# Three users of two PSUM banks in the expert stage of a hybrid decoder layer: one bank each for tables, layout products and turned halves

## The chip, the cores and the metric

The kernel runs on one core of a Trainium2 chip. The metric is the device time of one launch in microseconds. A core has a matrix engine (TensorE, rows "PE" for its multiplications and "PEld" for its weight loads), a vector engine (VectorE, "DVE"), a scalar engine (ScalarE, "ACT"), GpSimd ("POOL") and SyncE ("SP"), and 16 DMA engines that move data between HBM and the on-chip memory SBUF. Each engine works through its own list of instructions in order. TensorE writes its results to PSUM, a small memory of eight banks, each of 512 float32 values in every one of 128 partitions. VectorE and ScalarE read and write PSUM too.

## The reference, cut to what matters

One layer of a decoder for 512 prompt tokens and 64 sample tokens, width 2048. After a mixing block come the experts, the part that the change touches:

```
def peer(h, w_q, sub_keys, expert_u, expert_v):      # h: tokens x 2048
    ...
    q = (xb @ w_q).reshape(PEER_BLOCK, PEER_HEADS, 2, HALF_DIM)
    sc = jnp.einsum('thpk,pnk->thpn', q, sub_keys)
    v1, i1 = lax.top_k(sc[:, :, 0], PEER_TOPK)
    v2, i2 = lax.top_k(sc[:, :, 1], PEER_TOPK)
    ...                                              # the best 16 of the 256 pairs, for each of 8 heads
    g = jax.nn.softmax(top, axis=-1)
    act = jax.nn.gelu(jnp.einsum('td,thkd->thk', xb, expert_u[eidx])) * g
    return jnp.einsum('thk,thkd->td', act, expert_v[eidx])
```

Each token picks 128 of 16384 experts, and an expert is one row of `expert_u` and one of `expert_v`, each of 2048 float32 values.

## The kernel before

**Stages.** The first third computes the modulation, the projections, the two convolutions, the scan and the output projection. Then come the queries and the choice of experts. The rest is two long loops. The U loop (`for n in range(NU2)`, L2029, 144 rounds) multiplies all prompt tokens with 72 blocks of 128 experts each from the u table; the V loop (L2141) does the same with the v table, weighted. 48 of the 72 blocks (`NF`) are whole blocks of the table, taken by how often they are picked; the other 24 are put together from lists of single experts. Picks that fall into no block, and those of the sample tokens, are computed row by row: 198 gathered tiles of 128 u rows (one row of 2048 values for each of 128 partitions), each multiplied and summed against the tokens on VectorE (`dot`, L1553 to L1559), and as many of v rows.

**A half block.** Each block is two half blocks, so round `n` stands for block `i = n // 2` and half `c = n % 2`. `u_half` (L1691) issues 24 matmuls of 128x512, eight values of `kk` with three products each (high part times high, high times low, low times high, to keep float32 accuracy). The two halves of a block accumulate in one bank, `pu`, taken from a pair of banks with the tag "u". After the second half ScalarE applies gelu to the bank (L1710) and sends the result to HBM. The half block's data `raw` are split into high and low parts by ScalarE (`xhi`, L997) and GpSimd (`xlo`, L998). `ahead(n + 3, n + 2)` at the top of round `n` asks for the load of half block n+3 and splits half block n+2.

**Turned halves.** The 24 listed blocks arrive through an indirect DMA that GpSimd issues (`fetch_x`, L949, after `u_half` of round n for half block n+5, into two buffers `nat`), with experts in the partitions, and have to be turned. `turn_x` (L955) does so inside `u_half` of round n for half block n+3: two 128x128 transposes on TensorE, then a copy by ScalarE to `raw`, at `kk` = 1, 3, 5 and 7. This happens from round 93 on.

**Layout products.** For the V loop every prompt token's 128 gate weights are laid out as a table of 72 blocks x 128 experts. `g_pair` (L1964) makes one-hot operands for eight tokens on VectorE: `ops` compares the table `gk["o"]` with each pick's number inside its block (L1979), `eq` compares the table `gk["w"]` with the pick's block (L1980), and three products with the weights `gk["wq"]` give `wr` (L1982). All three tables lie in PSUM. `g_mm` (L1985) multiplies them, 12 small matmuls for four tokens, into `gk["g"]`, and `g_out` (L1994) has ScalarE copy the result to `stg`, which goes to HBM. `g_one` (L2022) calls both, at the top of a round and at `kk` = 2, 4 and 6, for pairs that were made at least one round earlier.

**Which bank holds what.** `g_start` (L1948) takes the two banks with the tag "g". The bank `kb` holds the tables `o` and `w` and the layout products `g`. The bank `tb` (named "tpbank") holds the weights `wq` and the turned halves `tp`. The program framework puts in the waits between engines: two accesses of one PSUM tile on different engines, which fill the same bank, are kept in the order of the program, whether or not they touch the same columns. The order on each engine is the one written here (`manual_schedule`, L1081), and the shares of each kind of work per round come from constants (`PIECE_G`, `RATE`, `PAIRS`, `LAG`).

Of the kernel before, what the change touches and what calls it, by code (L numbers as in the profile page):

```python
# [11 lines left out]
AF = mybir.ActivationFunctionType  # L12
# [21 lines left out]
L = 72  # L34
# [30 lines left out]
WP = 3  # L65
# [32 lines left out]
def build(ctx, tc, A, O, dbg=None):  # L98
    nc = tc.nc
    V, S, PE, G = nc.vector, nc.scalar, nc.tensor, nc.gpsimd  # L100
# [21 lines left out]
    ident = const.tile([128, 128], F32, name="ident")  # L122
# [302 lines left out]
    for n in ("lru_wa", "lru_wx"):  # L425
        g = wk.tile([128, KW, 64], F32, name=f"g_{n}")
# [28 lines left out]
    def project(src, nm):  # L455
        his, los = stream_w(src, nm)
        p = pp.tile([128, 2, 512], F32, name=f"pp_{nm}", tag="pp")
        mm3([p[:, 0, :HT], p[:, 1, :HT]], his, los, movs)
        return p
# [183 lines left out]
    for k in range(KD):  # L643
        if k < 2:
            out_half(k, 1)
            p = p_out[k]
        else:
            p = project(A["w_out"][k], f"o{k}")
# [25 lines left out]
    def pbank(tag, nm, bufs):  # L674
        return psum["p"].tile([128, 512], F32, name=nm, tag=tag, bufs=bufs)
# [7 lines left out]
    for q in range(4):  # L683
        modulate(x1, R, None, 3, 4 * q, 4, "h2")
        mm3(pq0, *w_q, movs, range(4 * q, 4 * q + 4))
        t = adap.tile([128, 4, 512], F32, name=f"h2s{q}", tag="wa")
# [202 lines left out]
    def new_row(nm):  # L889
        s_ = free_slot()  # L890
        if s_ is None:
            s_ = min(range(slots_now[0]), key=lambda x: held_by[x])
        k = held_by[s_] = len(row_log)
        row_log.append(False)
        return (gp if s_ < RB else pools["vx"]).tile([128, D], F32, name=nm, tag=f"row{s_}", bufs=1), k
# [4 lines left out]
    for i in range(RB):  # L900
        r, k = new_row(f"row0_{i}")
# [35 lines left out]
    nat = {}  # L937
    raws, parts, gsb, ahl, acts, pools = {}, {}, {}, {}, {}, {}
# [16 lines left out]
    def turn_x(n, a):  # L955
        if n not in nat:
            return
        if a == 0:
            k = n % 3
            raws[n] = (ws if k < 2 else wx).tile([128, 8, 128], F32, name=f"raw{n}", tag="wraw", bufs=2 if k < 2 else 1)  # L960
        tp = gk["tp"] if "tp" in gk else pbank("g", f"tp{n}_{a}", 2)[:, :256]
        src = nat[n] if a < 3 else nat.pop(n)
        for k in range(2):
            PE.transpose(tp[:, k * 128:(k + 1) * 128], src[:, (2 * a + k) * 128:(2 * a + k + 1) * 128], ident)  # L964
        S.activation(raws[n][:, 2 * a:2 * a + 2, :], tp.rearrange("p (k c) -> p k c", c=128), AF.Copy)

    def load(n):
        if n >= len(stream):
# [292 lines left out]
    def look():  # L1261

        lp = pools.get("lp")
        if lp is None or "acc" not in lk:
            return
        if lk["feat"] and (len(lk["feat"]) > 1 or lk["next"] >= lk["lim"]):
            j, f = lk["feat"].pop(0)
            reg = lk["acc"][:, 0:256].rearrange("p (d r w) -> p d r w", d=4, w=8)
            for z in range(QT):
                PE.matmul(reg[:, :, 4 * (j % 2) + z, :], f[:, z * 128:(z + 1) * 128], lk["tab"], start=True, stop=True)  # L1270
            if j % JC == 0:
                lk["ev", j // JC] = lp.tile([128, 4, 4 * JC, 8], BF16, name=f"ev{j // JC}", tag="ev", bufs=2)
            if j % 2:
                S.activation(lk["ev", j // JC][:, :, 4 * (j % JC) - 4:4 * (j % JC) + 4, :], reg, AF.Copy)
                lk["done"] = j + 1
        if lk["next"] < lk["lim"]:
            j = lk["next"]
            lk["next"] += 1
            PE.matmul(lk["bc"], lk["one"][:, j:j + 1].to_broadcast([128, 128]), lk["kT", j // 64], start=True, stop=True)
            f = lp.tile([128, NA], F16, name=f"ft_{j}", tag="feat", bufs=3)  # L1280
            S.activation(f, lk["bc"], AF.Sign, bias=lk["bias"])
            lk["feat"].append((j, f))
# [179 lines left out]
    def pick_keys(R, nm, pool, iota1, b):  # L1462

        kk = pool.tile([128, 3, NPK], F32, name=f"kk{nm}", tag="kk", bufs=1)
        b = b.bitcast(U32).rearrange("p (a k) -> p a k", a=2)
        V.tensor_scalar(b[:, 0, :], R[:, 1, :].bitcast(U32), 16, None, op0=ALU.logical_shift_right)
        V.tensor_scalar(b[:, 1, :], R[:, 1, :].bitcast(U32), 65535, None, op0=ALU.bitwise_and)
        V.tensor_copy(kk[:, 1:, :], b)
        for a in range(3):
            V.scalar_tensor_tensor(kk[:, a, :], iota1, 65536.0 if a else 16384.0, kk[:, a, :] if a else R[:, 0, :],  # L1470
                                   op0=ALU.mult, op1=ALU.add)
            V.scalar_tensor_tensor(kk[:, a, :], R[:, 0, :], 0.5, kk[:, a, :], op0=ALU.is_gt, op1=ALU.mult)
        return kk
# [207 lines left out]
    fin = {}  # L1681
# [3 lines left out]
    def mid(n):  # L1685
        for f in mids.pop(n, ()):
            f()
        if R1 is not None and "o" in gk:
            g_one(n)

    def u_half(n, i, c):  # L1691
        hi, lo = parts.pop(n)
        if c == 0:
            fin["pu"] = pbank("u", f"pu{i}", 2)
        pu = fin["pu"]
        for kk in range(8):
            k = 8 * c + kk
            if kk < LK:
                look()
            if kk % 2:  # L1700
                turn_x(n + 3, kk // 2)
            if kk in (2, 6) and R1 is not None and "o" in gk:
                g_one(n)
            if kk == 4:
                mid(n)
            for a, (st, mv) in enumerate(((hi, 0), (hi, 1), (lo, 0))):
                PE.matmul(pu, st[:, kk, :], movA[mv](k), start=k == 0 and a == 0, stop=k == KD - 1 and a == 2)  # L1707
        if c == 1:
            act = actp.tile([128, NA], F32, name=f"act{i}", tag="act", bufs=2)
            S.activation(act, pu, AF.Gelu_apprx_tanh)  # L1710
            nc.scalar.dma_start(actd[V_AT[i] // SG][:, V_AT[i] % SG, :], act)
# [3 lines left out]
    def v_column(n, gi, q, bl, first, last, kq):  # L1715

        k = q * (KD // VQ) + kq
        if first:
            pvs[k] = pbank("ug"[kq // 2], f"pv{gi}_{k}", 2)
        pv = pvs[k]  # L1720
        end = gi == len(GROUPS) - 1
        for j, i in enumerate(bl):
            hi, lo = parts[n + j // 2]
            ah, al = ahl[i]
            hi, lo = (x.rearrange("p (a k) c -> p a k c", a=2)[:, j % 2, kq, :] for x in (hi, lo))
            for a, (st, mv) in enumerate(((hi, ah), (hi, al), (lo, ah))):
                PE.matmul(pv, st, mv, start=first and j == 0 and a == 0,  # L1727
                          stop=last and not end and j == SG - 1 and a == 2)
        if end:
            for t in range(QT):  # L1730
                PE.matmul(pv[:, t * 128:(t + 1) * 128], fin["tok"][t][:, k * 128:(k + 1) * 128], ident,  # L1731
                          start=False, stop=t == QT - 1)
        return k, pv
# [208 lines left out]
    gk = {}  # L1942
# [5 lines left out]
    def g_start():  # L1948

        kb = pbank("g", "kb", 2)  # L1950
        tb = pbank("g", "tpbank", 2)
        cw = pools["rg"].tile([128, 4, L, 2], BF16, name="cw", tag="eq", bufs=1)[:, 0]
        co = pools["rg"].tile([128, 4, 128, 2], BF16, name="co", tag="op", bufs=PAIRS // 2)[:, 0]
        S.activation(cw, nd["ordr"][:, :, None].to_broadcast([128, L, 2]), AF.Copy)
        S.activation(co, iota[:, :, None].to_broadcast([128, 128, 2]), AF.Copy)
        S.activation(kb[:, :128], co.rearrange("p i t -> p (i t)").bitcast(F32), AF.Copy)
        S.activation(kb[:, 128:128 + L], cw.rearrange("p i t -> p (i t)").bitcast(F32), AF.Copy)
        gk["o"] = kb[:, :128].bitcast(BF16).rearrange("p (i b) -> p i b", b=2)
        gk["w"] = kb[:, 128:128 + L].bitcast(BF16).rearrange("p (i b) -> p i b", b=2)
        gk["g"] = kb[:, 128 + L:128 + 5 * L]  # L1960
        gk["wq"] = tb[:, 256:256 + 64 * WP].rearrange("p (w t) -> p w t", w=WP)
        gk["tp"] = tb[:, :256]

    def g_pair(b):  # L1964

# [56 lines left out]
    def g_one(n):  # L2022
        nonlocal spare
        if n >= R1 + FIRST_G and gm[1] < min(upto(n - LAG), gm[2]):
            g_out(gm[1], g_mm(gm[1]))
            gm[1] += 1
            spare += 0.4

    for n in range(NU2):  # L2029
        _, i, c = stream[n]  # L2030
# [110 lines left out]
    for m in range(M):  # L2141
        gi, q, bl, first, final = steps[m]
        n = NU2 + 2 * m
# [4 lines left out]
        for kq in range(KD // VQ):  # L2148
# [9 lines left out]
            if (m, kq) in tplan:  # L2158
                t = len(fin["tok"])
# [5 lines left out]
            k, pv = v_column(n, gi, q, bl, first, final, kq)  # L2165
# [33 lines left out]
    with tc.If(any_ > 0), tc.tile_pool(name="fb", bufs=1) as fp:  # L2199
        io1 = fp.tile([128, 128], F32, name="f_io1")  # L2200
        V.tensor_scalar(io1, iota, 1.0, None, op0=ALU.add)
        for i, (p0, n, c) in enumerate(GT):
# [7 lines left out]
            kb = fp.tile([128, 2 * NPK], F32, name=f"kbf{i}", tag="kb", bufs=1)  # L2210
            kk = pick_keys(R_, f"f{i}", fp, io1, kb)
            w = kk[:, 1, :]
# [9 lines left out]
            a = fp.tile([128, D], F32, name=f"f_a{i}", tag="a", bufs=1)  # L2222
# [105 lines left out]
```

## Time and profile before

| | us |
|---|---|
| median of 3 runs | 3469.14 (3460.91 to 3477.18) |
| the profiled execution | 3474.89 |
| its span, first to last instruction | 3473.0 |
| TensorE matmuls busy | 3087.6 (89%) |
| VectorE busy | 2120.8 (61%) |
| GpSimd busy | 1801.5 (52%) |
| ScalarE busy | 1052.9 (30%) |

In the views of the trace a row names a line of the kernel, the engine and what it writes from what it reads. "Idle" is the time in which that engine had stood still just before the instruction, and the name behind the arrow is the instruction whose end released it; "issue" stands there where the profile shows no releaser. A view by stretches gives, for each stretch of the span in microseconds, every engine's busy time, the clock that TensorE was granted (1 is full speed), the share of time that the DMA engines were busy and the rate at which data moved. Matmuls overlap in TensorE, so that the sum of their durations says less than the distance from one start to the next.

### The profile page before, as it was taken

The numbers are of one execution on the slowest core, as the hardware profiler recorded it, in microseconds if no ns is written. First come the engines' busy times: TensorE is split into PE (matmuls) and PEld (weight loads), VectorE is DVE, ScalarE is ACT, GpSimd is POOL, SyncE is SP. The second block draws the span as 40 slices with busy tenths as digits, with TensorE's granted clock in tenths as the row PEclk, the third lists the DMA queues.
The fourth block names the chain that finished last, engine by engine and source line by source line (L and its number), as shares of the span: only waits on it lengthen the run. The fifth ranks groups of instructions, "written<-read, shape, count | busy, mean of one in ns | idle before, by whom it ended". The sixth has DMA issues, their size and how long they took to land. (4 is left out here: it accounts for less than half of the span.)

```text
span 3473.0 us, 48158 instructions
## 1 busy us (share of the span) xinstructions
PE 3087.6 (89%) x18277; PEld 2535.7 (73%) x18277; DVE 2120.8 (61%) x3550; ACT 1052.9 (30%) x1540; POOL 1801.5 (52%) x1136
## 2 busy tenths in 40 slices
PE   6999999999999899798877777778889998988997
PEld 3788889999899886567766655556667876767776
DVE  3456321232458879787866645555657777877765
ACT  3344211232332336552222333333332221211122
POOL 2333333443432353346534434345679988888872
PEclk8999999999999999899988888799999999999998
DMA  9644566533331264458865766567989999989994
GB/s 389 245 140 141 199 208 213 168 117 133 108 103 62 74 217 171 140 170 309 318 248 191 274 202 203 170 220 274 368 289 381 395 382 406 377 338 384 353 341 159
DMA packets 270862, 831.74 MB, mean 239 GB/s; under 512 B 32476, under 2 KB 70236, under 8 KB 222332
## 3 DMA queue, kind: packets, MB, share of 16 engines
q0 software_dynamic: 73728, 437.74, 33.5%
q1 hardware_dynamic: 132960, 313.27, 26.1%
q10 hardware_dynamic: 63936, 77.61, 6.4%
q8 instruction: 144, 2.36, 0.3%
q14 instruction: 94, 0.77, 0.1%
HBM read 806.49 MB, written 62.61 MB: 250 GB/s over the span
## 5 line engine op out<-in xcount | busy, mean ns | idle before, releaser
L998 POOL TENSOR_TENSOR xlo<-raw,xhi 128x1024 fp32r<-128x1024 f32 x288 | 697.0, 2432 | 486.8 <-ACT xhi L997 466.1
L1586 DVE SCALAR_TENSOR_TENSOR accB<-v,dots,accB 128x2048 f32<-128x2048 f32 x186 | 437.7, 2353 | 186.9 <-DMA v<-v,rows 185.7
L1707 PE MATMUL pu<-hhi,xhi 128*128 128x512 f32 x1152 | 542.5, 471 | 0.0
L997 ACT ACTIVATE xhi<-raw 128x1024 fp32r<-128x1024 f32 x288 | 302.1, 1058 | 783.9 <-PE pv L1727 293.2
L1559 DVE SCALAR_TENSOR_TENSOR u<-u,hT 128x2048 f32<-128x2048 f32 x198 | 447.6, 2281 | 129.7 <-DMA u<-u,rows 116.9
L1727 PE MATMUL pv<-ahi,xhi 128*128 128x512 f32 x1152 | 468.7, 407 | 51.7 <-DVE acc L1749 43.9
L1727 PE MATMUL pv<-ahi,xlo 128*128 128x512 f32 x1152 | 465.0, 404 | 17.5 <-POOL xlo L998 17.4
L1707 PE MATMUL pu<-hlo,xhi 128*128 128x512 f32 x1152 | 479.7, 416 | 0.0
L1707 PE MATMUL pu<-hhi,xlo 128*128 128x512 f32 x1152 | 478.3, 415 | 0.0
L1727 PE MATMUL pv<-alo,xhi 128*128 128x512 f32 x1152 | 463.6, 402 | 0.0
L1727 PEld LDWEIGHTS pv<-ahi,xhi 128*128 128x128 f32 x1152 | 222.4, 193 | 113.4 <-issue 35.4
L1727 PEld LDWEIGHTS pv<-ahi,xlo 128*128 128x128 f32 x1152 | 222.0, 193 | 77.8 <-POOL xlo L998 25.6
L1707 PEld LDWEIGHTS pu<-hhi,xlo 128*128 128x128 f32 x1152 | 233.8, 203 | 55.7
L1707 PEld LDWEIGHTS pu<-hhi,xhi 128*128 128x128 f32 x1152 | 235.5, 204 | 44.4 <-issue 8.6
L1707 PEld LDWEIGHTS pu<-hlo,xhi 128*128 128x128 f32 x1152 | 236.9, 206 | 34.8
L1727 PEld LDWEIGHTS pv<-alo,xhi 128*128 128x128 f32 x1152 | 222.8, 193 | 51.0
L1531 POOL DMA_INDIRECT v<-v,rows x198 | 208.6, 1053 | 57.6 <-issue 40.6
L1531 POOL DMA_INDIRECT u<-u,rows x198 | 205.2, 1036 | 60.9 <-issue 26.0
L964 PE MATMUL tpbank<-ident,nat 128*128 128x128 f32 x384 | 83.7, 304 | 131.2 <-issue 108.4
L1979 DVE TENSOR_TENSOR op<-kb,kw 128x1024 bf16<-128x1024 bf16 x64 | 44.1, 690 | 252.7 <-ACT stg L1998 252.7
L964 PEld LDWEIGHTS tpbank<-ident,nat 128*128 128x128 f32 x384 | 55.3, 155 | 173.6 <-issue 139.7
L946 POOL DMA_INDIRECT nat<-u,lists x48 | 47.7, 993 | 214.9 <-PE tpbank L964 210.9
(628 smaller groups left out, 6241.4 us busy)
## 6 DMA issues: line engine op xcount, KB each, us to landing
wa<-w_ada SPq DMA_DIRECT2D x96, 1024.0 KB, 7.2
raw<-ut SPq DMA_DIRECT2D x96, 512.0 KB, 4.2
raw<-v SPq DMA_DIRECT2D x192, 256.0 KB, 8.0
actd<-act ACTq DMA_DIRECT2D x72, 256.0 KB, 4.6
gd<-stg ACTq DMA_DIRECT2D x64, 288.0 KB, 5.0
gsb<-gd ACTq DMA_DIRECT2D x72, 256.0 KB, 17.3
actr<-actd ACTq DMA_DIRECT2D x36, 512.0 KB, 8.7
raw_o<-w_out SPq DMA_DIRECT2D x32, 512.0 KB, 3.6
```

What stands on the lines that cost most here:

```text
L946: G.indirect_dma_start(out=out, out_offset=None, in_=src, in_offset=bass.IndirectOffsetOnAxis(ap=idx, axis=0), bounds_check=NE * 128 * n - ...
L964: PE.transpose(tp[:, k * 128:(k + 1) * 128], src[:, (2 * a + k) * 128:(2 * a + k + 1) * 128], ident)
L997: S.activation(hi, raw, AF.Copy)
L998: G.tensor_sub(lo, raw, r32(hi))
L1531: G.indirect_dma_start(out=out, out_offset=None, in_=src, in_offset=bass.IndirectOffsetOnAxis(ap=idx, axis=0), bounds_check=NE * 128 - 1, ...
L1559: V.scalar_tensor_tensor(r, r, 1.0, st["h"], op0=ALU.mult, op1=ALU.mult, accum_out=dots[i][:, j:j + 1])
L1586: V.scalar_tensor_tensor(st["a"], r, dots[i][:, j:j + 1], st["a"], op0=ALU.mult, op1=ALU.add)
L1707: PE.matmul(pu, st[:, kk, :], movA[mv](k), start=k == 0 and a == 0, stop=k == KD - 1 and a == 2)
L1727: PE.matmul(pv, st, mv, start=first and j == 0 and a == 0, stop=last and not end and j == SG - 1 and a == 2)
L1979: V.tensor_tensor(ops, gk["o"][:, None, :, :].to_broadcast([128, 4, 128, 2]), two(spare_t(1)[:, z, t], 128), op=ALU.is_equal)
```

## The change

Three parts, none of which changes what is computed.

- `kb` now holds the three tables only (`o`, `w` and `wq`, the last at its end). The bank that was `tb` holds the layout products only (`gbank`).
- The turned halves go to a bank of the "u" pair: that of the *next* block, `fin["pun"]`, which is now taken one block ahead, at the first half of the block before. When that block begins, its first matmul starts the accumulation afresh in the same bank.
- The turns come four at a time, at `kk` = 2 and 5, with one copy of 128x512 behind each four, in place of two at a time at `kk` = 1, 3, 5 and 7 with copies of 128x256.

```
     def turn_x(n, a):
...
-        tp = gk["tp"] if "tp" in gk else pbank("g", f"tp{n}_{a}", 2)[:, :256]
-        src = nat[n] if a < 3 else nat.pop(n)
-        for k in range(2):
-            PE.transpose(tp[:, k * 128:(k + 1) * 128], src[:, (2 * a + k) * 128:(2 * a + k + 1) * 128], ident)
-        S.activation(raws[n][:, 2 * a:2 * a + 2, :], tp.rearrange("p (k c) -> p k c", c=128), AF.Copy)
+        tp = fin["pun"]
+        src = nat[n] if a == 0 else nat.pop(n)
+        for k in range(4):
+            PE.transpose(tp[:, k * 128:(k + 1) * 128], src[:, (4 * a + k) * 128:(4 * a + k + 1) * 128], ident)
+        S.activation(raws[n][:, 4 * a:4 * a + 4, :], tp.rearrange("p (k c) -> p k c", c=128), AF.Copy)
...
     def u_half(n, i, c):
         hi, lo = parts.pop(n)
         if c == 0:
-            fin["pu"] = pbank("u", f"pu{i}", 2)
+            fin["pu"] = fin.pop("pun") if i else pbank("u", "pu0", 2)
+            if i + 1 < L:
+                fin["pun"] = pbank("u", f"pu{i + 1}", 2)
...
-            if kk % 2:
-                turn_x(n + 3, kk // 2)
+            if kk in (2, 5):
+                turn_x(n + 3, kk // 4)
...
     def g_start():
         kb = pbank("g", "kb", 2)
-        tb = pbank("g", "tpbank", 2)
+        gk["g"] = pbank("g", "gbank", 2)[:, :4 * L]
...
-        gk["g"] = kb[:, 128 + L:128 + 5 * L]
-        gk["wq"] = tb[:, 256:256 + 64 * WP].rearrange("p (w t) -> p w t", w=WP)
-        gk["tp"] = tb[:, :256]
+        gk["wq"] = kb[:, 512 - 64 * WP:].rearrange("p (w t) -> p w t", w=WP)
```

## The prediction

> **What bounds the kernel now.** I read the stretches of the U loop first, to see which stage runs below its own pace, then the waits of those stages, then the order of time in one round.
>
> ```profile
> core 0: us, PE busy (x) PEld busy (x) DVE busy (x) ACT busy (x) POOL busy (x), PEclk, DMA share, GB/s
> 1460.00:1700.00 240.00, 224.12 (x1219) 172.32 (x1218) 181.89 (x255) 91.23 (x141) 128.79 (x80) 0.96 0.68 253
> 1700.00:1965.00 265.00, 209.58 (x1304) 160.88 (x1302) 191.78 (x377) 72.82 (x96) 114.01 (x77) 0.86 0.68 245
> 1965.00:2405.00 440.00, 325.87 (x2031) 245.23 (x2031) 232.34 (x401) 150.37 (x271) 180.94 (x133) 0.85 0.62 211
> 2405.00:2510.00 105.00, 87.19 (x406) 67.21 (x405) 64.36 (x53) 37.32 (x69) 73.91 (x54) 0.97 0.96 356
> ```
>
> The middle two rows are the stages with layout products: stage A (1700 to 1965) without turned halves, stage B (1965 to 2405) with them. In both no engine and no DMA is full, and the granted clock is 0.86 and 0.85 against 0.96 and 0.97 around them. Something makes the engines take turns. The same stretches for the U matmuls alone say how many half blocks each did (24 matmuls make one):
>
> ```profile
> 1460.00:1700.00 240.00, 209.79 (x819) 155.69 (x819) 0.96 0.68 253
> 1700.00:1965.00 265.00, 190.26 (x656) 138.15 (x654) 0.86 0.68 245
> 1965.00:2405.00 440.00, 289.87 (x857) 170.15 (x857) 0.85 0.62 211
> 2405.00:2510.00 105.00, 84.88 (x308) 55.68 (x307) 0.97 0.96 356
> ```
>
> That is 34.1, 27.3, 35.7 and 12.8 half blocks, at 7.0, 9.7, 12.3 and 8.2 us each. The waits of stage A, then of stage B:
>
> ```profile
> DVE op L1979 <- ACT stg L1998: 63.7, 17, 6.8
> PE kb L1991 <- DVE eq L1980: 55.4, 25, 7.8
> ```
>
> ```profile
> DVE op L1979 <- ACT stg L1998: 189.0, 33, 9.8
> PE tpbank L964 <- issue: 108.4, 32, 6.1
> ```
>
> VectorE waits for ScalarE's copy of the layout product, although `op` reads only the table and the copy only the products: both lie in `kb`. In stage A TensorE then waits for VectorE's reading of the table before it may write the next product into `kb`. In stage B TensorE waits before a turn, and the releaser is not named. The order of time names it:
>
> ```profile
> 2249.63 0.64 ACT L1998 ACTIVATE stg<-kb 128x288 f32<-128x288 f32 x1
> ...
> 2250.31 0.69 DVE L1979 TENSOR_TENSOR op<-kb,kw 128x1024 bf16<-128x1024 bf16 x1 [5.64 <-ACT stg L1998]
> 2250.92 0.45 DVE L1980 TENSOR_TENSOR eq<-kb,kw 128x576 bf16<-128x576 bf16 x1
> 2251.40 1.18 DVE L1982 TENSOR_TENSOR wr<-eq,tpbank 128x576 bf16<-128x576 bf16 x3
> ...
> 2252.68 0.41 PE L964 MATMUL tpbank<-ident,nat 128*128 128x128 f32 x2 [2.67 <-issue]
> ```
>
> The copy ends at 2250.27 and `op` starts at 2250.31; the third `wr` ends at 2252.58 and the turn starts at 2252.68. `wr` reads the weights in `tpbank`, the bank that the turn writes. So each round runs through a ring: product on TensorE, copy on ScalarE, one-hots on VectorE, turn on TensorE. It is a ring of banks and not of data, since the products use pairs made a round or more earlier.
>
> **What the waits cost TensorE.** Standing still: 55.4 us in A; in B 108.4. Beside it, what follows a pause is slow:
>
> ```profile
> 1816.94 0.57 PE L1991 MATMUL kb<-wr,op 128*128 128x72 bf16 x12 [1.88 <-DVE eq L1980]
> ...
> 1818.58 0.63 PE L1707 MATMUL pu<-hlo,xhi 128*128 128x512 f32 x1
> 1819.00 0.63 PE L1707 MATMUL pu<-hhi,xlo 128*128 128x512 f32 x1
> ```
>
> Starts here lie 0.42 us apart, after a pause of 1.88 us. Undisturbed they lie 0.23 apart, from 2258.49 to 2258.72 in the next rows of the same engine, which show the price of a turn and of a product too:
>
> ```profile
> 2258.04 0.38 PE L964 MATMUL tpbank<-ident,nat 128*128 128x128 f32 x2
> ...
> 2258.49 0.40 PE L1707 MATMUL pu<-hlo,xhi 128*128 128x512 f32 x1
> 2258.72 0.40 PE L1707 MATMUL pu<-hhi,xlo 128*128 128x512 f32 x1
> 2258.96 0.57 PE L1991 MATMUL kb<-wr,op 128*128 128x72 bf16 x12
> ...
> 2259.69 0.40 PE L1707 MATMUL pu<-hlo,xhi 128*128 128x512 f32 x1
> ```
>
> Two turns take 2258.49 - 2258.04 less one matmul, 0.22 us. A product of 12 takes 2259.69 - 2258.72 less two matmuls, 0.51. Turns are 4 x 35.7 = 143 pairs in B. The products are counted here, in A and in B, one matmul in twelve:
>
> ```profile
> 1700.00:1965.00 265.00, 33.24 (x648) 26.24 (x648) 0.86 0.68 245
> 1965.00:2405.00 440.00, 52.29 (x888) 41.86 (x888) 0.85 0.62 211
> ```
>
> TensorE's floor is then, in A, 656 x 0.23 + 54 x 0.51 = 151 + 28 = 179 us, 6.5 per half block; in B, 857 x 0.23 + 143 x 0.22 + 74 x 0.51 = 197 + 31 + 38 = 266 us, 7.5 per half block. Over the two stages 445 of 705 us. Of the excess of 260 us, 164 is standing still and the rest, 96, mostly the slow clock behind it.
>
> **The change part by part.**
>
> *Tables alone in `kb`.* After the first fill only VectorE touches that bank, so `op` no longer waits for the copy and the product no longer for `eq`. Gone: the 55.4 us of A. What is next late for the product is its data, one round old; for `op` it is the operand buffer, freed by an older product, which is issued at the latest at the top of the round. VectorE may still pause there, but TensorE doesn't wait on that.
>
> *Turned halves in the bank of the next block.* The turn no longer waits for `wr`: gone are the 108.4 us of B. Three waits come in its place, all on ScalarE. The first four turns of a block wait for the gelu of the block before, whose bank they use. The order of time on ScalarE at a round's top:
>
> ```profile
> 2259.16 0.60 ACT L1710 ACTIVATE act<-pu 128x512 f32<-128x512 f32 x1 [0.32 <-PE pu L1707]
> ...
> 2260.16 1.06 ACT L997 ACTIVATE xhi<-raw 128x1024 fp32r<-128x1024 f32 x1 [0.40 <-ACT act L1710]
> ```
>
> The gelu ends at 2259.76, 0.8 us after the block's last matmul has made room at 2258.96, and it stands ahead of `xhi` in ScalarE's list; the turns come six matmuls later, 1.4 us, with a product more. The second four wait for the first copy, nine matmuls later, 2.1 us. The next block's first matmul waits for the last copy, nine matmuls and a product after the turns. Behind a waiting turn stand all the matmuls of the round. The nearest rows for what such waits cost are those of the last stretch, where the turned bank has ScalarE as its only other user:
>
> ```profile
> PE tpbank L964 <- DMA nat<-u,lists: 13.6, 7, 3.6
> PE tpbank L964 <- ACT raw L965: 3.9, 4, 1.6
> ```
>
> 3.9 us in 12.8 half blocks is 0.3 each, 14 us over the 48 turned half blocks, and that is my upper bound for a mild case; the lower is a small gain, since two waits per half block replace four. I take nothing, as the distances are longer than before.
>
> *Four at a time.* The number of turns stays. ScalarE makes two copies of 128x512 (0.60 each by the gelu's row, same shape) in place of four of 128x256, on an engine that was busy 150.37 of B's 440 us: worth nothing. `nat` is needed one triple of matmuls, 3 x 0.23 = 0.7 us, later and is free two triples, 1.4 us, earlier, so GpSimd's fetch of half block n+5, which waits for the last turn with everything behind it on GpSimd, goes out earlier. In the last stretch that takes up to 0.7 us off each of 7 waits: 4 us gained.
>
> **What is next late.** The stages will not reach TensorE's floor. VectorE was busy 191.8 us in A and 232.3 in B, the DMA engines 0.68 x 265 = 180 and 0.62 x 440 = 273 us, and that work stays. So A cannot go below 192, nor B below 273. The stretch ahead, with VectorE at 76% and DMA at 0.68, runs 7.0 us per half block for 24 x 0.23 = 5.5 of U matmuls, 1.5 more (its other matmuls included); the last one, with DMA at 0.96, 8.2 for 5.5 + 4 x 0.22 = 6.4, 1.8 more. I take 1.5 for A, as VectorE would be 88% busy: 8.0 x 27.3 = 218 us. For B, 1.2, because VectorE has room and DMA would be at 0.88: 8.7 x 35.7 = 311 us. Gain: 265 - 218 = 47 in A, 440 - 311 = 129 in B, 4 behind, together 180 us. With the excess at 0.5 A meets VectorE's 192 and B 286, a gain of 231; with 1.8 the sums are 227 and 332, a gain of 150.
>
> Part of this hangs on the clock. The Trainium skill (TensorE: Matmul & The Clock Gate, "Why this matters for your kernels") warns of pauses above about 3 us. By that alone A's pauses, 55.4 / 25 = 2.2 us on average, would mostly cost no clock, and the gain in A would lose up to 265 - 179 - 55 = 31 us. The trace doesn't agree: 0.86 in A, and the slow row after 1.88 us. I go by the trace.
>
> The profiled execution took 3474.9 us, 1.9 more than its span and 5.8 more than the median. 3474.9 - 180 = 3295, or 3289 against the median; I say 3290.
>
> **The rivals.**
>
> *Rows become the bound* (same sign, smaller). VectorE works in order, and if it has to wait for gathered rows it brings one-hots late. In the stretch with DMA at 0.96 it did:
>
> ```profile
> DVE u L1559 <- DMA u<-u,rows: 37.6, 21, 4.3
> ```
>
> That is 2.9 us per half block. On top of VectorE's own 424 us / 63 = 6.7 it makes 9.6 x 63 = 605 us for the two stages, a gain of 100 + 4: 3365. For it: DMA rises to 0.85 and over. Against: it rises there without the extra loads of the last stretch (356 GB/s against 211 and 245).
>
> *The ring closes elsewhere* (no change): the waits of the same length reappear at the turns, because `nat` or the operand buffers are late. Then 3465. Against it: the fetch leaves earlier, and the pairs have a round in hand.
>
> *The turned bank stalls the accumulation* (slower). If ScalarE comes late with gelu or a copy, TensorE stops in front of a turn or in front of a block's first matmul, where before no U matmul depended on a turn's copy. The Trainium skill (PSUM — Partial Sum Buffer, "PSUM bank collisions raise a hardware error") asks for just this guard: accesses of two engines to one bank are kept apart whatever columns they touch. The price is the delay times 48 half blocks. It cancels the gain from 180 / 48 = 3.8 us per half block, and is measurably slower from 4.1. ScalarE's whole queue at the top of a round, gelu 0.60, `xhi` 1.06, `stg` 0.64 (the row at 2249.63), is 2.3 us, so it would have to wait for something itself. With 4.3 us per half block it ends at 3495.
>
> **How the numbers follow.** The measurement can tell about 0.5%, 17 us, from no change. Forecast (gain 150 to 231, up to 240 with TensorE near its floor): 0.64, and 0.03 for more. Rows the bound (gain 60 to 150): 0.25. No change: 0.04. Slower: 0.04. The range goes from 3225 (a gain of 240) to 3390, which takes in most of the second case. Faster 0.92, same 0.04, slower 0.04.
>
> **What would show it.** Right: stage A and B together take about 530 us, not 705; no wait of `op` for `stg`, of a product for `eq`, or of a turn without a named releaser; a granted clock near 0.95 in both; DMA near 0.85; the stretches before 1700 and in the V loop unchanged. Wrong: the clock stays at 0.86; turns wait for `nat` or copies by more than 1 us per half block; U matmuls wait for `raw`'s copy; or VectorE stands still for `u` rows by over 100 us.

## The result, and the profile after

The changed kernel takes 3241.33 us (median of 4 runs, 3239.04 to 3243.22), the kernel before 3472.23 (4 runs, 3460.91 to 3477.18): a ratio of 0.9339, with a 95% interval of 0.9314 to 0.9364. The forecast was 3290 in a range of 3225 to 3390.

Where it went is read between four landmarks that both traces have: the first one-hots (`op`, L1979), the first turn, the last layout product and the last turn (L964, L1991). They bound stage A, stage B, the last stretch of the U loop and the rest. The profiled executions:

| | A | B | last stretch | rest | span |
|---|---|---|---|---|---|
| before | 267.1 | 435.3 | 103.3 | 966.6 | 3473.0 |
| after | 195.0 | 281.5 | 98.7 | 965.8 | 3241.4 |
| difference | -72.1 | -153.8 | -4.6 | -0.8 | -231.6 |

So all but 6 us lies in the two stages. This is the view by stretches of the kernel after: the stretch ahead, A, B and the last one (length, then busy time with instructions of TensorE's matmuls, its weight loads, VectorE, ScalarE and GpSimd, then granted clock, DMA share and GB/s):

```profile
1460.00:1700.00 240.00, 223.71 (x1221) 172.33 (x1221) 184.98 (x258) 91.19 (x141) 128.49 (x81) 0.97 0.68 254
1700.00:1895.00 195.00, 179.65 (x1305) 141.00 (x1303) 191.90 (x371) 74.07 (x96) 116.15 (x77) 1.00 0.87 329
1895.00:2177.00 282.00, 268.17 (x2019) 216.06 (x2020) 234.78 (x403) 134.64 (x197) 181.26 (x133) 0.99 0.89 327
2177.00:2276.00 99.00, 85.77 (x395) 68.53 (x394) 61.71 (x52) 32.72 (x45) 69.39 (x52) 0.93 0.96 366
```

Both stages now have a clock of 0.99 and over, against 0.86 and 0.85. VectorE and DMA do the same work in less time. In A the longest wait is GpSimd's for a row buffer that VectorE still reads, and TensorE has one kind of wait only up to the first turn; the second block has the waits of B that concern TensorE and the one-hots:

```profile
POOL u L1531 <- DVE u L1559: 54.2, 24, 5.2
PE gbank L1991 <- ACT stg L1998: 12.2, 13, 1.1
```

```profile
DVE op L1979 <- PE gbank L1991: 30.2, 21, 3.4
PE gbank L1991 <- ACT stg L1998: 9.4, 15, 1.4
PE pu L964 <- DMA nat<-u,lists: 6.8, 3, 3.4
```

The waits of `op` for `stg`, of the product for `eq` and of the turn for an unnamed releaser are gone. What is left between TensorE and its neighbours is the product's wait for the copy of the product ahead of it, with which it shares a bank still, and it is short. The order of time in a round of B shows the new sequence:

```profile
1951.07 0.58 PE L1991 MATMUL gbank<-wr,op 128*128 128x72 bf16 x12
1951.27 0.60 ACT L1712 ACTIVATE act<-pu 128x512 f32<-128x512 f32 x1 [1.48 <-PE pu L1709]
...
1952.27 1.06 ACT L997 ACTIVATE xhi<-raw 128x1024 fp32r<-128x1024 f32 x1 [0.40 <-ACT act L1712]
...
1952.94 0.60 PE L964 MATMUL pu<-ident,nat 128*128 128x128 f32 x4
1953.23 0.64 ACT L1998 ACTIVATE stg<-gbank 128x288 f32<-128x288 f32 x1
...
1953.92 0.56 PE L1991 MATMUL gbank<-wr,op 128*128 128x72 bf16 x12 [0.38 <-ACT stg L1998]
...
1954.52 0.69 DVE L1979 TENSOR_TENSOR op<-kb,kw 128x1024 bf16<-128x1024 bf16 x1 [3.14 <-PE gbank L1991]
```

The gelu frees the turn's bank at 1951.87, 1.07 us ahead of the turns. ScalarE gives the first product's copy its turn only behind `xhi`, and the second product stands still for 0.38 us. VectorE waits 3.14 us for a product, because that frees an operand buffer; no row here waits for VectorE then.

### The profile page after: what moved, and what is told of

Same layout as the page of the kernel before. It is cut to its first block, busy times and chain, and to the rows that moved or that the text cites. A ratio compares the mean times of both kernels' runs of the same rounds, so it can differ in the third digit from the quotient of the medians.

```text
span 3241.4 us, 48042 instructions
## 1 busy us (share of the span) xinstructions
PE 2999.7 (93%) x18277; PEld 2490.7 (77%) x18277; DVE 2125.2 (66%) x3550; ACT 1035.8 (32%) x1444; POOL 1803.2 (56%) x1136
## 4 chain that ended last, share of the span: by engine, by line
PE 58%; DVE 15%; DMA 11%; POOL 7%; issue 5%; ACT 3%; ACTq 1%; SPq 0%; POOLq 0%; DVEq 0%
PE pu L1709 14%; PE pv L1729 9%; PE pp_o L156 6%; DMA v<-v,rows 5%; DVE u L1559 3%; PE pp_c L156 3%; PE pp_s L156 3%; PE pp_b L156 3%; PE qa L156 3%; PE qb L156 2%; PE ada L206 2%; PE pp_x L156 2%; PE pp_y L156 2%; DMA nat<-u,lists 2%; POOL xlo L998 2%
## 5 line engine op out<-in xcount | busy, mean ns | idle before, releaser
L1709 PE MATMUL pu<-hhi,xhi 128*128 128x512 f32 x1152 | 501.0, 435 | 0.0
L1709 PE MATMUL pu<-hhi,xlo 128*128 128x512 f32 x1152 | 457.1, 397 | 0.0
L1709 PE MATMUL pu<-hlo,xhi 128*128 128x512 f32 x1152 | 455.6, 396 | 0.0
L1709 PEld LDWEIGHTS pu<-hhi,xlo 128*128 128x128 f32 x1152 | 219.5, 191 | 50.2
L1709 PEld LDWEIGHTS pu<-hhi,xhi 128*128 128x128 f32 x1152 | 219.6, 191 | 46.9 <-issue 8.7
L1709 PEld LDWEIGHTS pu<-hlo,xhi 128*128 128x128 f32 x1152 | 220.3, 191 | 38.2
L145 POOL TENSOR_TENSOR wlo_q<-raw_q,whi_q 128x1024 fp32r<-128x1024 f32 x28 | 67.9, 2430 | 150.1 <-ACT whi_q L143 144.1
L145 POOL TENSOR_TENSOR wlo_o<-raw_o,whi_o 128x1024 fp32r<-128x1024 f32 x32 | 77.5, 2422 | 119.8 <-ACT whi_o L143 115.8
L206 PE MATMUL ada<-wa,cpad 128*32 128x512 f32 x768 | 103.1, 633 | 29.1 <-DMA wa<-w_ada 28.3
L946 POOL DMA_INDIRECT raw<-v,lists x96 | 104.4, 1087 | 22.7 <-POOL xlo L998 10.4
```

What stands on the lines that cost most here:

```text
L145: lo_engine(share).tensor_sub(lo, raw, r32(hi))
L206: PE.matmul(acc[32 * g:32 * g + 32, :], cpad[:, 4 * kq + g, :], w[:, g, :], start=kq == 0, stop=kq == 3)
L946: G.indirect_dma_start(out=out, out_offset=None, in_=src, in_offset=bass.IndirectOffsetOnAxis(ap=idx, axis=0), bounds_check=NE * 128 * n - ...
```

## The experiments

Stages are measured as above, each in one profiled execution; the medians are of 4 or 5 runs. Ratios are to the kernel before, timed beside each run; where the interval of one overlaps that of the changed kernel (0.9314 to 0.9364), the two are not clearly told apart. The first one-hots start anywhere from 1696.8 to 1704.7 us in these runs, though hardly an edit acts ahead of them, so a few us of one stage's length can be a shift of its ends.

| | median | A | B | last | rest |
|---|---|---|---|---|---|
| tables alone (e1) | 3294.79 | 196.3 | 323.6 | 105.1 | 970.0 |
| turns only (e2) | 3346.89 | 259.5 | 319.2 | 98.7 | 969.7 |
| two at a time (e3) | 3252.18 | 192.9 | 290.6 | 101.2 | 964.7 |
| weights with products (e4) | 3358.91 | 261.8 | 328.1 | 98.2 | 970.3 |
| `eq` twice (e5) | 3249.34 | 202.2 | 284.1 | 97.9 | 966.8 |
| before, kept busy (e7) | 3414.78 | 250.7 | 390.2 | 105.6 | 969.9 |
| tables in SBUF (e8) | 3286.52 | 238.2 | 283.5 | 98.1 | 966.0 |
| rows later (e9) | 3245.78 | 192.1 | 283.8 | 97.9 | 976.5 |
| slots slower (e10) | 3268.17 | 198.7 | 278.4 | 99.1 | 994.7 |
| product later (e11) | 3238.36 | 191.2 | 278.0 | 99.6 | 966.8 |
| rows and product (e12) | 3239.03 | 185.4 | 281.9 | 100.1 | 967.6 |

**Which part brings it.** The theory: a ring through VectorE, closed by shared banks. The rival: that the turned halves' place alone matters in B.

```
 kernel before, one part (e1):
-        gk["g"] = kb[:, 128 + L:128 + 5 * L]
-        gk["wq"] = tb[:, 256:256 + 64 * WP].rearrange("p (w t) -> p w t", w=WP)
-        gk["tp"] = tb[:, :256]
+        gk["g"] = tb[:, :4 * L]
+        gk["wq"] = kb[:, 512 - 64 * WP:].rearrange("p (w t) -> p w t", w=WP)
+        gk["tp"] = tb[:, 256:]
```

> The kernel before with one part of the change: the three tables alone in one bank; layout products and turned halves share the other, turns still two at a time. If the ring through VectorE is the cause, only ScalarE's copies stand between products and turns (copies of 0.64 and 0.38 us): stage A (first one-hots to first turn, 267 us before, 195 after) as after, 195; stage B (first turn to last product, 435 before, 282 after) at most 1 us per half block more than after, 285 to 318; in all 3245 to 3280. Rival, that the turned halves need a bank of their own as well: B stays near 400 us and the whole near 3365.

Ratio to before 0.9489 (0.9452 to 0.9527). A is as after. B is 42 us longer than after, a little more than the bound that I gave, and the median lies 15 us above the 3280 that I gave. One row says why, the waits of TensorE in B:

```profile
PE tpbank L964 <- ACT stg L1998: 38.2, 37, 2.8
```

The turn that follows a product at once waits for its copy, since both lie in one bank. The tables' part alone is worth about 178 of the 231 us.

```
 changed kernel, the other part alone (e2):
-        gk["g"] = pbank("g", "gbank", 2)[:, :4 * L]
+        tb = pbank("g", "tpbank", 2)
...
-        gk["wq"] = kb[:, 512 - 64 * WP:].rearrange("p (w t) -> p w t", w=WP)
+        gk["g"] = kb[:, 128 + L:128 + 5 * L]
+        gk["wq"] = tb[:, 256:256 + 64 * WP].rearrange("p (w t) -> p w t", w=WP)
```

> The other part alone: turned halves in the next block's bank, four at a time; the tables for one-hots stay with the layout products, as before. Ring theory: the product still waits for eq in every round, so stage A is as before, 267 us at a granted clock near 0.87; in stage B the wait of the turn is gone but that of the product comes in its place, as long as in A: 9.7 us per half block and 0.9 for the turns, about 375 us for B (435 before). In all about 3410. Rival, that the turn's wait was all that mattered in B: B near 285 us, in all about 3320.

Ratio 0.9636 (0.9597 to 0.9675). A is nearly as before, and so is its wait, but B is 319, between the two expectations and nearer to the rival's 285, as the median is to the rival's 3320. The product's waits for `eq`, in A and in B:

```profile
PE kb L1992 <- DVE eq L1981: 57.4, 25, 9.4
```

```profile
PE kb L1992 <- DVE eq L1981: 39.9, 33, 4.7
```

The wait did come back in B, in nearly every round, but at 1.2 us on average and not at A's 2.3, and the clock stays high with it. The rows by stretches of this kernel, A and B:

```profile
1698.80:1958.30 259.50, 202.09 (x1307) 156.05 (x1306) 191.57 (x374) 73.42 (x96) 114.31 (x77) 0.89 0.70 251
1958.30:2277.50 319.20, 276.26 (x2019) 219.38 (x2018) 229.81 (x399) 135.60 (x197) 180.88 (x133) 0.97 0.80 287
```

I had carried A's pause over to B. By an estimate the four turns that now stand ahead of the product give VectorE 0.4 us of B's difference (two turns took 0.22 in the trace before); the rest of it isn't settled by the runs. The parts don't add, 178 and 126 make more than 231, since either of them takes away the turn's wait for `wr`.

```
 changed kernel, weights moved to the products' bank (e4):
-        gk["g"] = pbank("g", "gbank", 2)[:, :4 * L]
+        gb = pbank("g", "gbank", 2)
+        gk["g"] = gb[:, :4 * L]
...
-        gk["wq"] = kb[:, 512 - 64 * WP:].rearrange("p (w t) -> p w t", w=WP)
+        gk["wq"] = gb[:, 512 - 64 * WP:].rearrange("p (w t) -> p w t", w=WP)
```

> The changed kernel with one table moved: the weights wq lie in the free end of the layout products' bank (columns 320 to 511; products in 0 to 287), the other two tables alone, turns as in the change. Ring theory: one table suffices to close the ring, now through wr, which is later on VectorE than eq by 1.1 us: stage A at least as long as before, 267 to 300 us, stage B 380 to 440, the clock near 0.86 in both, in all 3410 to 3500; wr waits for stg. Rival, that disjoint columns of one bank don't matter and something else in the change brought the gain: 3241.

Ratio 0.9672 (0.9635 to 0.9709). One table of three, in columns that no product touches, costs 118 us, half of the gain. Its rows of A:

```profile
PE gbank L1992 <- DVE wr L1983: 63.6, 25, 8.0
DVE wr L1983 <- ACT stg L1999: 45.7, 14, 6.3
```

So it is the bank that is guarded and not the columns: `wr` waits for a copy of other columns, and the product for `wr`. That is the rule of the Trainium skill (PSUM — Partial Sum Buffer, "PSUM bank collisions raise a hardware error"), at work here through the program's waits. A is a little below what I had put, B at 328 far below, and with it the whole, 51 us below 3410: the product's pauses in B are 1.4 us on average (46.8 us in 33), and the clock is 0.97 there and 0.91 in A.

```
 changed kernel, turns two at a time (e3):
+        tp = tp[:, 256 * (a % 2):256 * (a % 2) + 256]
+        src = nat[n] if a < 3 else nat.pop(n)
+        for k in range(2):
+            PE.transpose(tp[:, k * 128:(k + 1) * 128], src[:, (2 * a + k) * 128:(2 * a + k + 1) * 128], ident)
+        S.activation(raws[n][:, 2 * a:2 * a + 2, :], tp.rearrange("p (k c) -> p k c", c=128), AF.Copy)
...
+            if kk % 2:
+                turn_x(n + 3, kk // 2)
```

> The changed kernel with turns two at a time again, at kk 1, 3, 5 and 7, still in the next block's bank (halves of it in turn), four copies of 128x256. If only the choice of banks counts: within 0.5% of the changed kernel, 3235 to 3257, with up to 5 us more where nat is late, as it is needed 0.7 us earlier and free 1.4 us later. Rival, that batching four turns matters through the bank's waits for ScalarE: 20 us or more above 3241.

Ratio 0.9369 (0.9333 to 0.9405), 11 us above the changed kernel's median, B 9 us longer. The intervals overlap, though each of the four runs (3250.36 and more) is above each of the changed kernel's (3243.22 at most). So batching is worth some 10 us, if anything, and not 20. TensorE's named waits in B are 4 us longer and its matmuls busy for 4 us more (272.3 against 268.1); why the latter, stays open.

**What the clock is worth.**

```
 kernel before, matmuls that nobody reads ahead of the waiting ones (e7); "pun" is the next block's bank, taken as in the change:
+            if kk == 1 and n + 3 in nat and gm[0] < NB2:
+                keep_busy(fin["pun"], 10)
             if kk % 2:
                 turn_x(n + 3, kk // 2)
+            if kk == 2 and n + 3 not in nat and 0 < gm[1] < NB2:
+                keep_busy(fin["pun"], 8)
```

> The kernel before, its banks and waits unchanged, with TensorE kept busy in its pauses by matmuls that nobody reads (128x128, 0.21 us each): 8 ahead of the product at kk 2 in stage A, 10 ahead of the first turn of each half block in stage B, into the bank of the next block. They add 46 and 75 us of TensorE work. If the low clock comes from the pauses, the work lies inside them (55 and 108 us), the clock rises from 0.86 to 0.93 or more, and the slow matmuls (about 36 us in A, 60 in B) mostly go: A 245 to 260 (267 before), B 395 to 420 (435), in all 3415 to 3450. Rival, that the clock has another cause: it stays at 0.86 and the time rises by 0 to 40 us, 3470 to 3510.

Ratio 0.983 (0.9813 to 0.9846): 56 us less with every wait still in its place and with 126 us more of matmuls on TensorE. The median is at the low end of what I had put, and B a little below it. The rows by stretches, A and B:

```profile
1701.00:1951.70 250.70, 230.58 (x1721) 193.69 (x1719) 193.47 (x379) 74.00 (x96) 116.68 (x78) 0.98 0.72 261
1951.70:2341.90 390.20, 345.82 (x2641) 282.45 (x2642) 229.28 (x395) 150.24 (x268) 178.88 (x132) 0.99 0.69 235
```

The clock is 0.98 and 0.99. So the pauses were what lowered it, in A too. The average of A's 25 pauses, 2.2 us, hides their sizes: four are over 3 us (7.8 the longest), eleven lie between 1.88 and 1.97, and seven are under 1. A piece of the kernel before without a longer pause than 1.97, then a piece of B of the run with turns only, each with its waits:

```profile
1782.00:1839.00 57.00, 46.54 (x283) 35.42 (x282) 39.04 (x92) 16.00 (x21) 23.84 (x16) 0.85 0.69 245
PE kb L1991 <- DVE eq L1980: 10.5, 6, 2.0
```

```profile
2046.00:2143.00 97.00, 85.16 (x638) 67.72 (x637) 70.13 (x125) 42.79 (x62) 54.61 (x40) 1.00 0.73 261
PE kb L1992 <- DVE eq L1981: 11.8, 11, 1.7
```

Five pauses of 1.88 to 1.97 us and one of 0.84 go with a clock of 0.85, eleven of up to 1.71 with the full clock. The Trainium skill (TensorE: Matmul & The Clock Gate, "Why this matters for your kernels") sets the mark at pauses of about 3 us. The traces here put it lower, at 1.9 us or less.

**What bounds the changed kernel.**

```
 changed kernel (e5):
+        V.tensor_tensor(eq, gk["w"][:, None, :, :].to_broadcast([128, 4, L, 2]), two(spare_t(0)[:, z, t]), op=ALU.is_equal)
```

> The changed kernel with eq computed twice for each pair (same result): 64 times 0.447 us, 28.6 us more work on VectorE, 28 of the 64 in stage A. VectorE was busy 191.9 of A's 195 us and 235 of B's 282. If VectorE is now the bound in A and TensorE in B: A 12 us longer, B 0 to 5, in all 3253 to 3260. Rival, TensorE or DMA the bound in both: no change, 3238 to 3246. Rival, VectorE the bound in both: 28 us more, 3270.

Ratio 0.9359 (0.9346 to 0.9372), 8 us above the changed kernel with overlapping intervals, between the rival's 3246 and the 3253 that were expected of VectorE as A's bound. A grew by 7.2 us, and 4.5 of them are at its last instruction, the first turn, which waited 7.98 us for its half block here and 3.44 in the changed kernel:

```profile
1903.89 0.48 PE L964 MATMUL pu<-ident,nat 128*128 128x128 f32 x1 [7.98 <-DMA nat<-u,lists]
```

VectorE's work may reach TensorE by a detour: row buffers come free later, GpSimd waits for them, and the fetch of `nat` stands behind in its list. But the same wait is 6.7 us in the next run, where VectorE is busy for 180 us of A and not for 192, so the detour is argued and not shown. The next run takes VectorE work away instead, by planning 6.5 us of it per round.

```
-PIECE_G = 7.0
+PIECE_G = 6.5        (e10)
```

> The changed kernel with 6.5 us in place of 7.0 of VectorE work planned per round of stages A and B (TensorE's own floor is 6.5 per half block in A, 7.5 in B); what is put off is the sorting of slots, and with it the rows that wait for it. VectorE the bound in A: A 182 to 190; but the later end of the sorting leaves fewer rows done ahead of the V loop, where DMA is 98% busy, so the whole may keep 0 to 8 us of the 5 to 13: 3228 to 3245. If A stays at 195, VectorE isn't its bound.

Ratio 0.9416 (0.9397 to 0.9435), slower than the changed kernel by 27 us and outside the 3228 to 3245 that I had put. By the mark that I had set, VectorE isn't A's bound: A is 198.7 with VectorE busy for 180.

```profile
1698.50:1897.20 198.70, 180.28 (x1308) 141.61 (x1306) 180.11 (x342) 74.00 (x96) 115.03 (x75) 0.99 0.81 307
```

A is close to TensorE's floor instead: 179 us of its work, the product's waits of 12.2 and the first turn's of 3.4 make the 195 of the changed kernel, and with 10.9 and 6.7 here 197. VectorE, 98% busy in the changed kernel, is full beside it and doesn't set the end. The loss lies behind the U loop, 994.7 against 965.8 us, where the rows that came late have to be done: 25 of the 198 `dot`s come after 2275 us here and 16 in the changed kernel, and the last starts at 2396 us and not at 2350.

```
-            if kk in (2, 6) and R1 is not None and "o" in gk:
+            if kk in (3, 6) and R1 is not None and "o" in gk:      (e11)
```

> The changed kernel with the second chance for a layout product at kk 3 in place of kk 2, so that ScalarE has 0.7 us more for gelu, xhi and the copy of the first one. TensorE's waits for that copy (12.2 us in A, 9.4 in B) mostly go. B, where TensorE is the bound, 5 to 9 us shorter; A, where VectorE is, unchanged: 3232 to 3237. If it changes nothing, the waits lay in slack of B too: 3239 to 3243.

Ratio 0.9335 (0.9316 to 0.9353). TensorE's waits for the copy over A and B fall from 21.6 to 6.4 us:

```profile
PE pu L964 <- DMA nat<-u,lists: 12.4, 4, 6.8
PE gbank L1991 <- ACT stg L1998: 6.4, 17, 0.9
```

A and B are 3.8 and 3.5 us shorter, though nat's waits grow by 5.6; I had expected 5 to 9 in B and nothing in A. The median is 3 us below the changed kernel's, and the intervals overlap: not told apart.

```
-                due_g += RATE[R1 is not None] + ...
+                due_g += (RATE[0] if R1 is None else 1.4 if n < 2 * NF - 3 else 1.75) + ...      (e9; e12 has e11's edit too)
```

> The changed kernel with 1.4 u rows asked for per round in stage A and 1.75 in stage B, in place of 1.6 in both: about 4 tiles of rows (2.28 us each on VectorE) leave A for B. If VectorE is the bound in A (191.9 busy of 195 us) and TensorE in B: A 186 to 190, B 280 to 284, in all 3232 to 3238. Rival, TensorE or DMA the bound in A: no change, 3239 to 3243. Rival, the later rows run into B's bound: 3245 or more.

> The changed kernel with both edits, 1.4 and 1.75 rows per round and the product at kk 3. If they act on different stages they add: A 186 to 190, B 273 to 278, in all 3224 to 3232. If they share one bound, no better than the better of the two.

Ratios 0.9351 (0.9333 to 0.937) and 0.933 (0.9311 to 0.9348). A becomes 192.1 and, with both, 185.4 us, but 2.3 and 4.3 us of that is a later start (1702.7 and 1704.7 us against 1700.4), by which 12 and 20 U matmuls fewer fall into A. B is 283.8 and 281.9, and neither median is clear of 3241. The first is in the range of its second rival, 3245 or more (its profiled execution was its longest run, 3254.75), and the second is no better than the product's shift alone, so the two edits don't add. None of the variants beats the changed kernel by more than the measurement can tell.

**Why the tables are in PSUM at all.**

```
 changed kernel (e8): gk["o"] in perm, gk["w"] in ordr, both SBUF; in g_pair
-            V.tensor_tensor(wr[:, w], eq, two(gk["wq"][:, w, :].bitcast(BF16)[:, t]), op=ALU.mult)
+            V.tensor_tensor(wr[:, w], eq, two(spare_t(2 + w)[:, z, t]), op=ALU.mult)
```

> The changed kernel with the three tables in SBUF: two of them in tiles that have served their purpose, the weights read straight from the operand tile, without the 12 small copies. No bank is shared, so the ring stays open. If one-hots run as fast from SBUF (0.69, 0.45 and 0.45 us from PSUM): 3238 to 3246. If they run faster, by a fifth, VectorE has 0.5 us less per pair, 14 us less in stage A: 3226 to 3234. If reading SBUF twice puts VectorE in GpSimd's way, xlo (2.35 us) and one-hots get longer and A with them: 3250 to 3300.

Ratio 0.947 (0.9455 to 0.9484), 45 us slower than the changed kernel, 43 of them in A. The order of time shows `op` beside GpSimd's `xlo`:

```profile
1761.18 0.69 DVE L1972 TENSOR_TENSOR op<-perm,kw 128x1024 bf16<-128x1024 bf16 x1
...
1769.72 2.42 POOL L998 TENSOR_TENSOR xlo<-raw,xhi 128x1024 fp32r<-128x1024 f32 x1
...
1770.57 2.13 DVE L1972 TENSOR_TENSOR op<-perm,kw 128x1024 bf16<-128x1024 bf16 x1
```

Alone `op` takes 0.69 us as from PSUM; begun inside an `xlo`, it ends just after that does (1772.70 and 1772.14) and takes 2.13. The Trainium skill (SBUF — State Buffer, "Who interferes with whom") says that a VectorE instruction with two SBUF inputs contends with a GpSimd one that reads SBUF, and that the later one is blocked altogether; the rows agree. `xlo` itself doesn't get longer. `wr` loses more than `op`: in the first 195 us of A it takes 0.93 us on average and 0.45 from PSUM in the changed kernel. VectorE is busy for 235 of A's 238 us here, and TensorE waits 19.1 us for `wr`.

## Why the prediction was right, point by point

- *The ring of banks is what bounds the stages.* Shown: the run with one table in the products' bank closes it again, in A nearly to the old length (261.8 us) and in B in part (328.1 of 435.3), and the run with only the tables moved opens A altogether.
- *Standing still goes, 164 us.* Right; what took its place on TensorE is 6.8 us of waits for `nat` and 21.6 for the product's own copy, which I hadn't named. That wait was in the code before as well, hidden behind the ring.
- *The rest of TensorE's excess, 96 us, is mostly clock.* About 61 us of it, by the stage lengths of the kernel before with its pauses filled (16 in A, 45 in B; 56 by the medians). For A I went by the clock of 0.86 in the trace, and that run bears it out.
- *Three waits for ScalarE come in, at nothing.* Right: in both stages TensorE's turns wait for ScalarE's work for 0.2 us in all, and no U matmul waits for a turn's copy.
- *Four at a time at nothing, and 4 us for an earlier `nat`.* Perhaps too low: 11 us by the medians with the bank held fixed, with overlapping intervals.
- *What is next late: an excess over TensorE's floor of 1.5 us per half block in A and 1.2 in B.* This is the term that was mis-sized. Measured: (195.0 - 179) / 27.3 = 0.6 and (282 - 266) / 35.7 = 0.4. I had taken the excess from the stretches on either side, but the stretch ahead has TensorE work of its own in it that I counted as unrest (busy for 14 us beside the U matmuls, with 16 us in which it waits for its own data), and the last one stands still for `nat` under a DMA load of 0.96. So the gain was 231 us and not 180, and A and B took 477 us together and not 530. With the 0.5 that I set as the low end the sum gave 231 us, stage by stage too (73 and 154; 72.1 and 153.8 came), though it stopped A at VectorE's 192 us, which the run with less VectorE work doesn't bear out. I had also shaded the forecast for VectorE at 88% and DMA at 0.88; they went to 98% and 0.89 and cost next to nothing: no wait of TensorE in A names VectorE, as a round's one-hots aren't needed before the next round. Nor was 273 us a floor for B by DMA: the same 92 to 93 MB (211 x 440 and 327 x 282) took 0.62 x 440 = 273 us of the DMA engines' time before and 0.89 x 282 = 251 after.
- *Rivals.* Rows were not the bound: VectorE waited 14 us for them in B. The ring didn't close elsewhere, and the turned bank didn't stall the accumulation.

## What to carry to other kernels

Look for engines that take turns without any data between them: if an instruction waits for one with which it has no data in common, as `op` did for `stg`, see whether operands of the two share a PSUM bank. Separating them by who touches them, constants for one engine apart from results that pass between two, may open the ring. Price the opened stage by the floor of the engine that was held up, with only the waits that its own data still need, and not by the unrest of neighbouring stages with other loads. And count the pauses on TensorE twice: filling them with idle matmuls alone, every wait kept, was worth 56 us here, a quarter of the gain.

## What the runs showed of the hardware that was not expected

- Pauses of 1.88 to 1.97 us, one in about 10 us, took TensorE's granted clock to 0.85 over 57 us without a longer one; pauses of up to 1.71 us left it at 1.00 over 97 us; matmuls without use in the pauses brought it from 0.86 and 0.85 to 0.98 and 0.99 in the two stages.
- VectorE ran 98% busy over 195 us beside TensorE near its floor, a clock of 1.00 and DMA at 0.87; TensorE waited 12.2 us for ScalarE, 3.4 for DMA and not for VectorE.
- `op` with both inputs in SBUF took 0.69 us alone and 2.13 us beside a GpSimd instruction of 2.42; with one input in PSUM it never took more than 0.692 in the changed kernel.
